# Two of the opening modulation products from rounded halves, ScalarE taking norm work, S5 eigenvalues moved into the head and the first retention moved behind the first gate

## The chip, the cores and the metric

The kernel runs on one core of one Trainium2 chip. The metric is device time in microseconds (us); shown is the median of three runs.

## The reference, cut to what matters

One layer of a hybrid decoder, for a prompt of 2048 rows and 64 sample rows (8 sequences of 8), width 1024, all in float32.

```python
mod = silu(c) @ w_ada + b_ada                      # 9 rows of c, w_ada 1024 x 6144
sh1, sc1, gt1, sh2, sc2, gt2 = split(mod, 6)
h = rms_norm(x, norm1_g) * (1 + sc1) + sh1
q, k, v, g, u, gate_r, gate_s = split(h @ w_in)    # 512 x5, 1024, 1024
ret = silu(g) * rms_normalize(retention(rotary(q), rotary(k), v))
lam_bar = exp(lam * exp(log_dt)); b_bar = ((lam_bar - 1) / lam) * b
ssm = gelu(s5_scan(u, lam_bar, b_bar, c, d)); ssm *= sigmoid(ssm @ w_glu)
x = x + gt1 * ((sigmoid(gate_r) * (ret @ w_br) + sigmoid(gate_s) * (ssm @ w_bs)) @ w_out)
x = x + gt2 * (relu((rms_norm(x, norm2_g) * (1 + sc2) + sh2) @ w_up)**2 @ w_down)
```

## The kernel before

The prompt is worked in four super-blocks of 512 rows. `setup` is the head: it computes the modulation columns that the first norm needs (`ada0` to `ada3`, 512 columns of `w_ada` each; 0 and 1 are the shift, 2 and 3 the scale), normalises the first 512 rows of x and leaves them transposed as `hh` (rounded to fp32r) and `hl` (what the rounding left), two tiles of four 128-row chunks each. Each super-block then multiplies by `w_in` in blocks of 512 columns, in the order u, q, k, v, g, gr0, gs0, gr1, gs1, and goes on with `glu`, the branches, the output product and the MLP. Between the blocks of super-block 0 lie the remaining modulation products `ada4` to `ada11`.

A weight unit is 256 rows by 512 columns. `fetch` (L180) issues its load from SP's queue into one of four buffers `wraw`; `refill` has ScalarE (ACT) round it to `whi` (L190) and GpSimd (POOL) form `wlo = wraw - whi` (L193; VectorE, DVE, for the `ada` units). Five `whi`/`wlo` pairs exist (the ring). Each block has four units, and each unit 24 products on TensorE (PE): for each of four row blocks j, two chunks by hi·hi, hi·lo, lo·hi (L252), into four PSUM banks of the tag `pd`. The banks are evacuated after the fourth unit, and the next block needs them: for q and k that is three DVE multiplications a bank (L1552 to L1554, `qU`, `rt`).

In the head `ada0` to `ada3` are plain float32 products of 9 columns (L848); DVE adds the bias (`ba`, L881), PE turns the sum (`ptm`, L886) and DVE copies it to `modT` (L887). ACT squares x (L639, two halves a row block), DVE scales x by its reciprocal root (L863) and modulates it (`m`, L688), ACT rounds it to `hh` (L690), POOL forms `hl` (L691). `ada4` on are products of a 41-row stationary that holds c rounded and its rest with `whi` and `wlo` (L258): ACT copies one part out (L903), DVE adds bias and the other part (L905, L906), PE turns it (L912).

S5 work stands in generators: `spawn` puts one beside the blocks, and it goes a step further at fixed counts of `tick`, which the blocks call; `finish` runs it to its end. `s5_setup` computes the eigenvalue functions on DVE (tiles `s5w`, L978 to L1058), powers (`s5pw`), tables (`s5ca`, `s5sa`, L1113 to L1125), then in eight steps the block matrices (L1142 to L1158, PE's `pw`, `pk`); it must end after block k. `s5(0, 4)` is then the first scan, to be ended before the retention of super-block 0 begins, beside gr0.

What the code writes is not yet the order of each engine: a modelled scheduler orders each engine's queue when the program is built, and the engine then executes it strictly in that order. Calls of `refill(True)` keep their written place.

Of the kernel before, what the change touches and what calls it, by code (L numbers as in the profile page):

```python
# [81 lines left out]
class Layer:  # L82
# [688 lines left out]
    def setup(self):  # L771
# [59 lines left out]
        pg = self.bank("pg", [P, 16])  # L831
        nc.tensor.transpose(pg, gn, self.ident[:16, :16])
        z = self.unit("z", shape=(P, 8, 41))
        V.memset(z, 0.0)
        V.tensor_copy(self.cT, z)
        V.tensor_copy(z[:, :, 0:9], pt)
        nc.scalar.activation(self.cT[:, :, 0:9], z[:, :, 0:9], AF.Copy)
        V.tensor_sub(self.cT[:, :, 32:41], z[:, :, 0:9], self.cT[:, :, 0:9])
        V.tensor_copy(self.gT.rearrange("p a k -> p (a k)"), pg)
# [35 lines left out]
        self.late_setup = self.s5_setup()
        next(self.late_setup)

    def mod_out(self, n, p, bias):
        nc = self.nc
        t = self.work("mt", [9, 512])  # L880
        nc.vector.tensor_add(t, p, bias)  # L881
        if n in (4, 5, 10, 11):
            nc.sync.dma_start(self.modd[:, 512 * n:512 * n + 512], t)
        pt = self.pd.tile([P, 4, 9], F32, tag="pd", name="ptm")
        for a in range(4):
            nc.tensor.transpose(pt[:, a], t[:, a * P:a * P + P], self.ident[:9, :9])  # L886
        nc.vector.tensor_copy(self.modT[:, 4 * n:4 * n + 4], pt)  # L887
# [40 lines left out]
    def s5_setup(self):  # L928
# [19 lines left out]
        bc = self.unit("s5bc", shape=(P, 4, G, 16))  # L948
        Bb, Bs, Cn, Cs = (bc[:, a] for a in range(4))
        for a, (x0, x1) in ((0, ("ssm_b_re", "ssm_b_im")), (1, ("ssm_b_im", "ssm_b_re"))):  # L950
            nc.sync.dma_start(bc[0:64, a], i[x0][0].rearrange("g p m -> p g m"))
            nc.sync.dma_start(bc[64:P, a], i[x1][0].rearrange("g p m -> p g m"))
        cc = self.unit("s5cc", shape=(P, 4, 2, 2, 64))
        for a, (x0, x1) in ((0, ("ssm_c_re", "ssm_c_im")), (1, ("ssm_c_im", "ssm_c_re"))):
            for h, nm in ((0, x0), (1, x1)):
                nc.sync.dma_start(cc[:, :, a, h], i[nm][0].rearrange("(f g) m p -> (g m) f p", f=4))
        dcol = cst.tile([P, G], F32, name="dcol")
        V.memset(dcol, 0.0)
# [870 lines left out]
```

## Time and profile before

| | |
|---|---|
| median of 3 runs | 3049.08 us (3045.45 to 3052.35) |
| the profiled execution | 3046.86 us, of it 3045.0 us span on the core |
| mean granted TensorE clock | 0.971 |
| PE busy | 2901.0 us (95%) |
| DVE, ACT, POOL busy | 1805.9 (59%), 1413.8 (46%), 1729.9 us (57%) |
| chain that ended last | PE 75%, DVE 13%, DMA 4%, POOL 3% |

Over the whole span PE is the bound; the chain's DVE share says that there are places where PE waits. The change touches the head and super-block 0 up to `glu`, the first 400 us.

### The profile page before, as it was taken

The numbers are of one execution on the slowest core, as the hardware profiler recorded it, in microseconds if no ns is written. First come the engines' busy times: TensorE is split into PE (matmuls) and PEld (weight loads), VectorE is DVE, ScalarE is ACT, GpSimd is POOL, SyncE is SP. The second block draws the span as 40 slices with busy tenths as digits, with TensorE's granted clock in tenths as the row PEclk, the third lists the DMA queues.
The fourth block names the chain that finished last, engine by engine and source line by source line (L and its number), as shares of the span: only waits on it lengthen the run. The fifth ranks groups of instructions, "written<-read, shape, count | busy, mean of one in ns | idle before, by whom it ended". The sixth has DMA issues, their size and how long they took to land.

```text
span 3045.0 us, 37372 instructions
## 1 busy us (share of the span) xinstructions
PE 2901.0 (95%) x13436; PEld 2374.9 (78%) x13436; DVE 1805.9 (59%) x2937; ACT 1413.8 (46%) x2296; POOL 1729.9 (57%) x1036
## 2 busy tenths in 40 slices
PE   8789999999999899999999999999999999999997
PEld 4568777788778788887788778887888788877886
DVE  6978544770575776365842645555556755545556
ACT  3223463322454334644344345556764555567643
POOL 3331355434254734564445487668777666689772
PEclk9889999999999999999999999999999999999999
DMA  8475435643226954447644455556545644457542
GB/s 266 137 219 188 127 129 176 182 114 119 77 95 204 289 177 118 139 166 228 194 129 149 163 185 185 189 196 209 181 153 175 208 167 152 153 197 241 191 149 97
DMA packets 337325, 518.62 MB, mean 170 GB/s; under 512 B 72038, under 2 KB 168822, under 8 KB 333035
## 3 DMA queue, kind: packets, MB, share of 16 engines
q1 hardware_dynamic: 337140, 516.24, 52.3%
q8 instruction: 106, 1.74, 0.2%
q14 instruction: 79, 0.65, 0.1%
HBM read 401.39 MB, written 114.78 MB: 170 GB/s over the span
## 4 chain that ended last, share of the span: by engine, by line
PE 75%; DVE 13%; DMA 4%; POOL 3%; issue 2%; ACT 2%; SPq 0%; ACTq 0%; DVEq 0%; POOLq 0%
PE pq_up L408 18%; PE pq_down L408 16%; PE pd_gr L252 6%; PE pd_gs L252 5%; PE pd_wo L252 4%; PE pd_br L252 3%; PE pd_u L252 2%; PE pd_g L252 2%; PE pd_bs L252 2%; PE pd_k L252 2%; PE pd_q L252 2%; PE pd_v L252 2%; PE pd_glu L252 2%; POOL tw L310 1%; DVE s5t L1226 1%
## 5 line engine op out<-in xcount | busy, mean ns | idle before, releaser
L193 POOL TENSOR_TENSOR wlo<-wraw,whi 128x1024 fp32r<-128x1024 f32 x248 | 623.2, 2525 | 714.2 <-ACT whi L190 600.5
L190 ACT ACTIVATE whi<-wraw 128x1024 fp32r<-128x1024 f32 x312 | 324.2, 1058 | 575.1 <-PE pd_wo L252 55.0
L408 PE MATMUL pq_down<-shi,tw 128*128 128x512 f32 x1792 | 562.1, 393 | 13.9 <-ACT acc L466 9.7
L408 PE MATMUL pq_up<-shi,tw 128*128 128x512 f32 x1792 | 557.6, 391 | 10.6 <-ACT tw L309 7.5
L408 PEld LDWEIGHTS pq_down<-shi,tw 128*128 128x128 f32 x1792 | 339.1, 189 | 86.7 <-ACT acc L466 10.5
L408 PEld LDWEIGHTS pq_up<-shi,tw 128*128 128x128 f32 x1792 | 338.3, 189 | 83.2 <-ACT tw L309 8.8
L310 POOL TENSOR_TENSOR tw<-traw,tw 128x512 fp32r<-128x512 f32 x192 | 277.8, 1459 | 142.7 <-ACT tw L309 142.5
L408 PE MATMUL pq_down<-slo,tw 128*128 128x512 f32 x896 | 351.8, 393 | 0.0
L408 PE MATMUL pq_up<-slo,tw 128*128 128x512 f32 x896 | 350.2, 391 | 0.0
L468 DVE SCALAR_TENSOR_TENSOR acc<-pq_down,modT,acc 128x512 f32<-128x512 f32 x224 | 162.4, 745 | 96.2 <-PE pq_down L408 95.9
L395 ACT ACTIVATE shi<-sw 128x1024 fp32r<-128x1024 f32 x140 | 147.2, 1058 | 152.8 <-DMA sw<-sd 100.2
L408 PEld LDWEIGHTS pq_down<-slo,tw 128*128 128x128 f32 x896 | 169.6, 189 | 34.4
L408 PEld LDWEIGHTS pq_up<-slo,tw 128*128 128x128 f32 x896 | 169.4, 189 | 34.6
L381 DVE TENSOR_TENSOR slo<-sw,far 128x512 fp32r<-128x512 f32 x160 | 103.8, 683 | 107.5 <-ACT far L380 92.2
L309 ACT ACTIVATE tw<-traw 128x512 fp32r<-128x512 f32 x224 | 137.8, 624 | 55.8 <-PE pq_down L408 38.4
L418 ACT ACTIVATE aq<-pq_up 128x512 f32<-128x512 f32 x128 | 72.7, 592 | 171.6 <-PE pq_up L408 171.6
L400 DVE TENSOR_TENSOR slo<-sw,shi 128x1024 fp32r<-128x1024 f32 x60 | 110.8, 1863 | 63.7 <-ACT shi L395 60.3
L193 DVE TENSOR_TENSOR wlo<-wraw,whi 128x1024 fp32r<-128x1024 f32 x64 | 90.9, 1421 | 74.3 <-ACT whi L190 69.9
L344 POOL TENSOR_TENSOR ts<-traw,ts 128x512 f32<-128x512 f32 x64 | 95.2, 1487 | 53.9 <-issue 48.9
L309 ACT ACTIVATE tw<-ts 128x512 fp32r<-128x512 f32 x128 | 80.2, 627 | 80.2 <-PE pq_up L408 70.9
L344 POOL TENSOR_TENSOR ts<-traw 128x512 f32<-128x512 f32 x64 | 87.3, 1365 | 45.6 <-DMA traw<-in_w_up_dram 27.3
L310 POOL TENSOR_TENSOR tw<-t,tw 128x512 fp32r<-128x512 f32 x64 | 89.9, 1412 | 40.0 <-ACT tw L309 39.9
(537 smaller groups left out, 6866.8 us busy)
## 6 DMA issues: line engine op xcount, KB each, us to landing
wraw<-in_w_in_dram SPq DMA_DIRECT2D x144, 512.0 KB
sw<-sd SPq DMA_DIRECT2D x112, 512.0 KB
s5p<-s5c SPq DMA_DIRECT2D x32, 1024.0 KB
traw<-in_w_up_dram SPq DMA_DIRECT2D x64, 512.0 KB
sd<-sq SPq DMA_DIRECT2D x32, 1024.0 KB
sd<-aq SPq DMA_DIRECT2D x32, 768.0 KB
traw<-in_w_down_dram SPq DMA_DIRECT2D x24, 1024.0 KB
wraw<-in_w_ada_dram SPq DMA_DIRECT2D x32, 512.0 KB
```

The source lines that it names most:

```text
L190: a = nc.scalar.activation(hi, raw, AF.Copy)
L193: l = eng.tensor_sub(lo, raw, hi)
L252: nc.tensor.matmul(banks[j], a, b, start=(k == 0 and z == 0), stop=(k == nk - 1 and z == 2))
L309: self.nc.scalar.activation(t[:, 0], x, AF.Copy)
L310: eng.tensor_sub(t[:, 1], x, t[:, 0])
L344: G.tensor_sub(x[p], l, x[m] if isinstance(m, int) else m)
L381: self.nc.vector.tensor_sub(d, a, c)
L395: nc.scalar.activation(hi[:, a], t, AF.Copy)
L400: V.tensor_sub(lo[:, a], t, hi[:, a])
L408: self.nc.tensor.matmul(bank, w, x, start=(first and a == 0 and z == 0), stop=(a == 3 and z == 2), skip_group_check=True)
L418: copy = lambda d, b: nc.scalar.activation(d, b, AF.Copy)
L468: V.scalar_tensor_tensor(d, b, g, d, op0=ALU.mult, op1=ALU.add)
```

## The change

- `b_ada` and the two norm gains come as one tile of 64 rows and one transpose; `modT` is set to the bias beforehand, and later sums are added to it (`sums`). The bias tile `ba` and the bias rows and additions of ada6 to ada9 go.
- `ada0` and `ada2` stay float32 products (`full`). `ada1` and `ada3` become 16 products each with `whi`/`wlo` halves (`split`, `halves`), whose rounding takes ring pairs, ACT time and, in turn, POOL and DVE time.
- Scaling x by its reciprocal root goes from DVE to ACT (`norm`, L892 after), as does the modulation of the first four chunks and of half of the others (L686 in place of L688).
- `ada3`'s sums and the second four chunks of `hh`/`hl` are made in `rest`, beside block u.
- `s5_setup` begins in the head: eigenvalues there, loads of B and C later. The rest of it and the first scan become one generator, `first_s5`, with shorter pauses, that must end after gr0; the retention of super-block 0 begins there.

```diff
+        gb = self.work("gb", [64, P])
+        dma(gb[0:48], raw_ap(i["b_ada"], 0, [[P, 48], [1, P]]))
...
         load(0)
-        self.x_rows(xu[0][:, 0], 0, 0)
-        dma(ba, raw_ap(i["b_ada"], 0, [[0, 9], [1, 2048]]))
-        self.x_rows(xu[0][:, 1], 0, 1)
+        self.x_rows(x[0], 0, 0)
+        next(s5)
+        self.x_rows(x[1], 0, 1)
         load(2)
         for j in range(2, 4):
-            self.x_rows(xu[1][:, j - 2], 0, j)
+            self.x_rows(x[j], 0, j)
         load(1)
+        self.fetch()
         load(3)
-        for _ in range(RAW):
+        for _ in range(RAW - 1):
...
+        V.tensor_copy(self.modT, pg[:, 0:48, None].to_broadcast([P, 48, 9]))
...
+        def split(n):
+            ws = []
+            for u in range(4):
+                raw = wa[2 * n + u // 2][:, 2 * (u % 2):2 * (u % 2) + 2]
+                hi = self.ring.tile([P, 2, 512], F32R, name="whi")
+                lo = self.ring.tile([P, 2, 512], F32R, name="wlo")
+                nc.scalar.activation(hi, raw, AF.Copy)
+                (V if u % 2 else nc.gpsimd).tensor_sub(lo, raw, hi)
+                ws.append((hi, lo))
+            return ws
+
+        def halves(n, ws):
+            pa = self.bank(f"ps_ada{n}", [P, 512])
+            for k in range(8):
+                for a in range(2):
+                    nc.tensor.matmul(pa[:41], self.cT[:, k], ws[k // 2][a][:, k % 2], start=(k == 0 and a == 0),
+                                     stop=(k == 7 and a == 1))
+            t = self.work("mt", [9, 512])
+            nc.scalar.activation(t, pa[32:41], AF.Copy)
+            V.tensor_add(t, t, pa[0:9])
+            return t
...
+        def sums(n, pt):
+            m = self.modT[:, 4 * n:4 * n + 4]
+            V.tensor_add(m, pt, m)
+            if n > 1:
+                self.scales(n)
+
+        def norm(j):
+            r = self.now(self.row_rstd(x[j]))
+            nc.scalar.activation(x[j], x[j], AF.Copy, scale=r)
...
-                for j in range(4):
-                    r = self.now(self.row_rstd(x[j]))
-                    V.tensor_scalar(x[j], x[j], r, None, op0=ALU.mult)
...
+            self.norm_out(pt, q, self.s1[:, :, 0], self.modT[:, 0:8, 0], self.hh, self.hl, j, nc.gpsimd, q and j % 2)
+        t = full(0)
+        norm(0)
+        next(s5)
+        norm(1)
+        sums(0, turn_mod(0, t))
+        pts = [turn(0, 0), turn(0, 1)]
+        next(s5)
+        t = full(2)
+        norm(2)
+        norm(3)
+        pts.append(turn(0, 2))
+        sums(2, turn_mod(2, t))
+        w1 = split(1)
+        for j in range(4):
+            out(pts[j] if j < 3 else turn(0, 3), 0, j)
+        next(s5)
+        self.refill(True)
+        t1 = halves(1, w1)
+        w3 = split(3)
+        pts = [turn(1, 0), turn(1, 1)]
+        sums(1, turn_mod(1, t1))
+        pts.append(turn(1, 2))
+        t3 = halves(3, w3)
+        self.refill(True)
+
+        def rest():
+            yield 2
+            p = turn_mod(3, t3)
+            yield 1
+            sums(3, p)
+            for j in range(2):
+                out(pts[j], 1, j)
+            yield 2
+            pts.append(turn(1, 3))
+            for j in range(2, 4):
+                out(pts[j], 1, j)
+            for _ in range(2):
+                self.refill(True)
+
+        self.late_setup = s5
+        self.rest = rest()
...
-            yield n // 5 + 1
+            yield n // 8 + 1
...
+    def first_s5(self):
+        yield from self.late_setup
+        yield 6
+        yield from self.s5(0, 4)
...
-            s5 = self.spawn(self.late_setup, 2)
+            self.spawn(self.rest, 1)
+            s5 = self.spawn(self.first_s5(), 5)
...
-        if b == 0:
-            self.finish(s5)
-            s5 = self.spawn(self.s5(b, 4), 13)
...
-        self.finish(s5)
-        rh, rl = self.unit("rh", F32R), self.unit("rl", F32R)
+        if b:
...
+            if not b and a == 0:
+                self.finish(s5)
+                rh, rl = begin()
```

Three places show what this makes of the engines' queues. On ACT, in the head, from the squares of x (`junk`) to the first half of u's first unit, before:

```order
L639 ACTIVATE junk,ss<-x_125 128x512 x4
L639 ACTIVATE junk,ss<-x_126 128x512 x4
L690 ACTIVATE hh<-m 128x4x128 x4
L190 ACTIVATE whi<-wraw 128x1024 x2
L690 ACTIVATE hh<-m 128x4x128 x4
```

and now (`x_126` holds row blocks 0 and 1, `x_127` blocks 2 and 3; `whi<-wa` are ada1's units, then ada3's; `ps_ada_303` is ada2's sum):

```order
L853 ACTIVATE mt<-ps_ada_303 9x512
L639 ACTIVATE junk,ss<-x_127 128x512 x2
L892 ACTIVATE x_126<-x_126,y 128x1024
L862 ACTIVATE whi<-wa 128x1024 x2
L639 ACTIVATE junk,ss<-x_127 128x512 x2
L862 ACTIVATE whi<-wa 128x1024 x2
L892 ACTIVATE x_127<-x_127,y 128x1024 x2
L686 ACTIVATE m<-pt,modT,s_108 128x128 x16
L690 ACTIVATE hh<-m 128x4x128 x4
L190 ACTIVATE whi<-wraw 128x1024
L862 ACTIVATE whi<-wa 128x1024 x4
L874 ACTIVATE mt<-ps_ada_438 9x512
```

ACT now has 16 modulations, four scalings and four roundings of `w_ada` ahead of u's first unit.

On PE, where `ada4` (`ps_ada_816` before, `ps_ada_858` now) stands against block u, before:

```order
L252 MATMUL pd_u<-hh,whi 128x512
L252 MATMUL pd_u<-hl,whi 128x512
L252 MATMUL pd_u<-hh,wlo 128x512
L258 MATMUL ps_ada_816<-whi,cT 41x512
L258 MATMUL ps_ada_816<-wlo,cT 41x512
```

and now:

```order
L252 MATMUL pd_u<-hh,wlo 128x512
L252 MATMUL pd_u<-hh,whi 128x512 x4
L258 MATMUL ps_ada_858<-whi,cT 41x512
L258 MATMUL ps_ada_858<-wlo,cT 41x512
L258 MATMUL ps_ada_858<-whi,cT 41x512
```

Before, ada4 stood behind the last product of u; now 12 of its 16 products stand ahead of the last 44 of u.

On DVE, at the evacuation of q's first two banks, before:

```order
L1148 TENSOR_TENSOR s5pk<-s5pk,s5bx 128x512
L1552 TENSOR_TENSOR qU<-pd_q,rot 128x512
L1553 TENSOR_TENSOR rt_1004<-pd_q,rot 64x512
L1554 TENSOR_TENSOR rt_1004<-pd_q,rot 64x512
L1142 TENSOR_TENSOR s5bx<-s5bc,s5pw 128x512
L1143 TENSOR_TENSOR s5bx<-s5bc,s5pw 128x512
L1145 TENSOR_TENSOR s5bx<-s5bc,s5pw 128x512
L1142 TENSOR_TENSOR s5bx<-s5bc,s5pw 128x512
L1143 TENSOR_TENSOR s5bx<-s5bc,s5pw 128x512
```

and now:

```order
L1175 TENSOR_TENSOR s5sa<-s5tm 128x32x32
L1190 TENSOR_TENSOR s5bc<-s5bc,s5pw 128x512
L193 TENSOR_TENSOR wlo<-wraw,whi 128x1024
L1177 TENSOR_SCALAR s5sa<-s5sa 64x2048
L1191 COPY s5bc<-s5bc 64x512
L1192 COPY s5bc<-s5bc 64x512
L1205 TENSOR_TENSOR s5bx<-s5bc,s5pw 128x512
L1207 TENSOR_TENSOR s5pk<-s5bc,s5pw 128x512
L1205 TENSOR_TENSOR s5bx<-s5bc,s5pw 128x512
L1207 TENSOR_TENSOR s5pk<-s5bc,s5pw 128x512
L1208 TENSOR_TENSOR s5bx<-s5bc,s5pw 128x512
L1622 TENSOR_TENSOR qU<-pd_q,rot 128x512
```

The eigenvalues are no longer among DVE's rows beside u, but the whole of the tables (`s5ca`, `s5sa`, before beside k) now stands ahead of q's evacuation.

Further on, on PE, the last step of the first S5 scan (`px`, L1212, and `py`, L1240 and L1241) stood among gr0's products before; now its last `px` and `py` stand between gr0's last product and gs0's first.

## Rows read from the trace of the kernel before

**Rows 1.** Busy time by stage: us, PE busy, PE's weight loads, DVE, ACT, POOL (instructions in brackets), granted clock, DMA share, GB/s. The stages are: the head, u with ada4, q, k, the rest of S5's setup with the start of v, the rest of v and g, the gates.
```profile
0.00:47.30 47.30, 36.27 (x121) 11.39 (x121) 21.37 (x76) 12.32 (x25) 10.27 (x10) 1.00 0.90 316
47.30:75.00 27.70, 27.70 (x126) 21.18 (x125) 26.93 (x97) 14.19 (x19) 12.53 (x7) 1.00 0.75 177
75.00:130.00 55.00, 37.10 (x152) 28.48 (x151) 54.38 (x127) 12.51 (x14) 25.06 (x12) 0.81 0.44 138
130.00:175.00 45.00, 41.34 (x191) 32.19 (x190) 44.06 (x69) 12.06 (x13) 17.10 (x9) 0.96 0.42 130
175.00:215.00 40.00, 31.25 (x145) 26.62 (x144) 26.69 (x44) 12.60 (x25) 2.54 (x2) 0.79 0.85 235
215.00:251.00 36.00, 33.37 (x191) 27.39 (x189) 32.32 (x69) 11.52 (x17) 10.26 (x4) 1.00 0.93 341
251.00:394.00 143.00, 136.24 (x697) 109.31 (x698) 86.78 (x187) 54.55 (x77) 49.38 (x23) 0.94 0.46 138
```
**Rows 2.** The waits of 47 to 394 us: engine, line, what it waited for: us in total, times, longest.
```profile
PE pd_k L252 <- DVE rt L1554: 10.2, 1, 10.2
PE pw L1154 <- DVE s5bx L1147: 8.0, 1, 8.0
```
**Rows 3.** The same columns as rows 1, for slices of 5 us around these waits.
```profile
85.00:90.00 5.00, 0.00 (x0) 0.00 (x0) 4.88 (x29) 0.00 (x0) 0.00 (x0) 0.50 0.00 0
90.00:95.00 5.00, 5.00 (x15) 4.07 (x16) 4.91 (x14) 0.00 (x0) 0.00 (x0) 0.52 0.53 153
115.00:120.00 5.00, 0.00 (x0) 0.00 (x0) 5.00 (x3) 0.59 (x1) 5.00 (x3) 0.87 0.53 136
190.00:195.00 5.00, 0.21 (x1) 0.24 (x2) 5.00 (x9) 0.00 (x0) 0.00 (x0) 0.54 0.81 308
195.00:200.00 5.00, 5.00 (x29) 5.00 (x29) 4.72 (x10) 1.20 (x2) 0.00 (x0) 0.50 0.00 0
```
**Rows 4.** The timeline of DVE and POOL beside u and q: start, us, engine, line, operation, output and input, count.
```profile
74.19 2.40 DVE L1033 TENSOR_SCALAR s5w<-s5w 128x64 f32<-128x64 f32 x1
83.67 0.21 DVE L989 SCALAR_TENSOR_TENSOR s5w<-s5w 128x64 f32<-128x64 f32 x1
72.29 11.27 POOL L193 TENSOR_TENSOR wlo<-wraw,whi 128x1024 fp32r<-128x1024 f32 x4 [12.19 <-ACT whi L190]
108.35 0.69 DVE L1553 TENSOR_TENSOR rt<-pd_q,rot 64x512 f32<-64x512 f32 x1
108.30 2.41 POOL L193 TENSOR_TENSOR wlo<-wraw,whi 128x1024 fp32r<-128x1024 f32 x1 [24.74 <-PE pw L1154]
```
**Rows 5.** The timeline of the head, PE (ada0, ada2, ada3; ada1 is left out; then u's first product) and ACT; same columns.
```profile
9.83 8.54 PE L848 MATMUL ps_ada<-wa,z 128*9 128x512 f32 x16 [1.25 <-DVE z L836]
19.48 7.04 PE L848 MATMUL ps_ada<-wa,z 128*9 128x512 f32 x16
...
39.16 7.03 PE L848 MATMUL ps_ada<-wa,z 128*9 128x512 f32 x16
47.31 0.50 PE L252 MATMUL pd_u<-hh,whi 128*128 128x512 f32 x1
21.66 0.63 ACT L639 ACTIVATE junk<-x 128x512 f32<-128x512 f32 x1 [5.42 <-DMA x<-in_x_prompt_dram]
38.69 1.99 ACT L190 ACTIVATE whi<-wraw 128x1024 fp32r<-128x1024 f32 x2
```
**Rows 6.** Groups of instructions of ACT, by line: count, busy us, mean ns of one, idle before and its releaser (the first over the whole span; the second for 0 to 251 us; the third is L666, the same operation as the moved scaling, later in the kernel: count, least, median and greatest ns, first and last start).
```profile
L686 ACT ACTIVATE m<-pt,modT,s 128x128 f32<-128x128 f32 x96 | 34.8, 468 | 13.5 <-PE pt L673 13.5
L190 ACT ACTIVATE whi<-wraw 128x1024 fp32r<-128x1024 f32 x41 | 42.1, 1055 | 72.9 <-DMA wraw<-in_w_ada_dram 21.4 <-PE pd_q L252 20.5 <-PE pd_v L252 20.1
L666 ACT ACTIVATE xr<-xr,y x12: 1132/1151/1154, 384.9 to 1312.4; 128x1024 f32<-128x1024 f32 x12
L690 ACT ACTIVATE hh<-m 128x512 fp32r<-128x512 f32 x8 | 5.1, 632 | 22.8 <-DVE m L688 22.8
```
**Rows 7.** POOL's products of 0 to 394 us, and a load that lands late: ACT's rounding of an ada unit and its wait.
```profile
L193 POOL TENSOR_TENSOR wlo<-wraw,whi 128x1024 fp32r<-128x1024 f32 x40 | 101.7, 2562 | 187.9 <-ACT whi L190 133.2 <-PE ps_ada L258 30.0 <-PE pw L1154 24.7
68.74 1.06 ACT L190 ACTIVATE whi<-wraw 128x1024 fp32r<-128x1024 f32 x1 [3.35 <-DMA wraw<-in_w_ada_dram]
```
**Rows 8.** PE's timeline at ada4, first and last product, and at the first products of gr0 and glu.
```profile
70.97 0.39 PE L258 MATMUL ps_ada<-whi,cT 128*41 128x512 f32 x1
74.41 0.40 PE L258 MATMUL ps_ada<-wlo,cT 128*41 128x512 f32 x1
249.81 0.50 PE L252 MATMUL pd_gr<-hh,whi 128*128 128x512 f32 x1 [1.20 <-DVE gU L1585]
398.36 0.98 PE L252 MATMUL pd_glu<-gh,whi 128*128 128x512 f32 x2 [0.18 <-ACT gh L1629]
```
**Rows 9.** DVE's timeline: the last evacuation of q and of k, two S5 products in a row and a `wlo`, the last three with no POOL work beside them.
```profile
127.69 0.68 DVE L1554 TENSOR_TENSOR rt<-pd_q,rot 64x512 f32<-64x512 f32 x1
162.95 0.68 DVE L1554 TENSOR_TENSOR rt<-pd_k,rot 64x512 f32<-64x512 f32 x1
187.35 0.68 DVE L1142 TENSOR_TENSOR s5bx<-s5bc,s5pw 128x512 f32<-128x512 f32 x1
187.95 0.68 DVE L1143 TENSOR_TENSOR s5bx<-s5bc,s5pw 128x512 f32<-128x512 f32 x1
132.45 1.21 DVE L193 TENSOR_TENSOR wlo<-wraw,whi 128x1024 fp32r<-128x1024 f32 x1
```

More of the change, by code (lines that the diff above doesn't have):

```diff
@@ L684, in norm_out @@
             k = 4 * q + a
-            if eng is nc.vector:
+            if not vec:
                 nc.scalar.activation(m[:, a], pt[:, a], AF.Identity, scale=s[:, k:k + 1], bias=b[:, k:k + 1])
@@ L830, in setup @@
             nc.tensor.transpose(pt[:, k], th[:, k * P:k * P + P], self.ident[:9, :9])
[L831 to L839, printed above, removed]
+        pg = self.bank("pg", [P, 64])
+        nc.tensor.transpose(pg, gb, self.ident[:64, :64])
+        z = self.work("z", [P, 8, 9])
+        zero = self.work("zero", [P, 8, 41])
+        V.memset(zero, 0.0)
+        V.tensor_copy(self.cT, zero)
+        V.tensor_scalar(z, pt, 0.5, None, op0=ALU.mult)
+        nc.scalar.activation(self.cT[:, :, 0:9], z, AF.Copy)
+        V.tensor_sub(self.cT[:, :, 32:41], z, self.cT[:, :, 0:9])
+        V.tensor_copy(self.modT, pg[:, 0:48, None].to_broadcast([P, 48, 9]))
+        V.tensor_copy(self.gT.rearrange("p a k -> p (a k)"), pg[:, 48:64])
         V.memset(self.R, 0.0)
@@ L873, in setup, with out @@
-        for _ in range(RING - 2):
-            self.refill(True)
[L875 to L887, printed above, removed]
+        def out(pt, q, j):
+            self.norm_out(pt, q, self.s1[:, :, 0], self.modT[:, 0:8, 0], self.hh, self.hl, j, nc.gpsimd, q and j % 2)
@@ L913, in evac @@
             yield 2
-            nc.vector.tensor_copy(self.modT[:, 4 * n:4 * n + 4], pt)
+            m = self.modT[:, 4 * n:4 * n + 4]
+            if rows:
+                nc.vector.tensor_copy(m, pt)
+            else:
+                nc.vector.tensor_add(m, pt, m)
             if n in (8, 9):
@@ L947, in s5_setup @@
         nc.sync.dma_start(ldt, raw_ap(i["ssm_log_dt"], 0, [[0, P], [1, G]]))
[L948 to L958, printed above, removed]
-        nc.sync.dma_start(dcol[112:P], i["ssm_d"][0].rearrange("g m -> m g"))
         yield
@@ L1029, in s5_setup @@
         yield
+        bc = self.unit("s5bc", shape=(P, 4, G, 16))
+        Bb, Bs, Cn, Cs = (bc[:, a] for a in range(4))
+        for a, (x0, x1) in ((0, ("ssm_b_re", "ssm_b_im")), (1, ("ssm_b_im", "ssm_b_re"))):
+            nc.sync.dma_start(bc[0:64, a], i[x0][0].rearrange("g p m -> p g m"))
+            nc.sync.dma_start(bc[64:P, a], i[x1][0].rearrange("g p m -> p g m"))
+        cc = self.unit("s5cc", shape=(P, 4, 2, 2, 64))
+        for a, (x0, x1) in ((0, ("ssm_c_re", "ssm_c_im")), (1, ("ssm_c_im", "ssm_c_re"))):
+            for h, nm in ((0, x0), (1, x1)):
+                nc.sync.dma_start(cc[:, :, a, h], i[nm][0].rearrange("(f g) m p -> (g m) f p", f=4))
+        dcol = cst.tile([P, G], F32, name="dcol")
+        V.memset(dcol, 0.0)
+        nc.sync.dma_start(dcol[112:P], i["ssm_d"][0].rearrange("g m -> m g"))
         for _ in range(3):
@@ L1129, in s5_setup @@
                               t.rearrange("p (s g) c -> p s (g c)", s=8))
+        for a, dst in ((0, Cn), (1, Cs)):
+            pc = self.bank("pc", [P, 4, P])
+            for f in range(4):
+                nc.tensor.transpose(pc[:, f], cc[:, f, a].rearrange("q h p -> q (h p)"), self.ident)
+            nc.scalar.activation(dst.rearrange("p g m -> p (g m)"), pc.rearrange("p f q -> p (f q)"), AF.Copy)
+        V.tensor_scalar(Cn[64:P], Cn[64:P], -1.0, None, op0=ALU.mult)
+        V.tensor_mul(t1, Bs, fi[:, :, None].to_broadcast(bsh))
+        V.tensor_mul(Bb, Bb, fr[:, :, None].to_broadcast(bsh))
+        V.tensor_add(Bb, Bb, t1)
+        V.tensor_copy(Bs[0:64], Bb[64:P])
+        V.tensor_copy(Bs[64:P], Bb[0:64])
         k0 = pw[:, 1536:2048].rearrange("p (g m) -> p g m", m=16)
@@ L1597, in super_block, with begin @@
             fr.append(self.spawn(self.retention_sample(zS, retS), 2))
-        fr.append(self.spawn(self.retention(b, qU, kU, vU, gU, rh, rl), 40 if smp else 2))
+        def begin():
+            rr = self.unit("rh", F32R), self.unit("rl", F32R)
+            fr.append(self.spawn(self.retention(b, qU, kU, vU, gU, *rr), 40 if smp else 2))
+            return rr
+        if b:
+            rh, rl = begin()
         gate = {}
@@ L1618, in super_block @@
             more_ada()
+            if not b and a == 0:
+                self.finish(s5)
+                rh, rl = begin()
         self.finish(*fr)
```

69 lines of the change are left out of this document (27 added, 42 removed).

## The prediction

> **What bounds the kernel now.** I read the table by stage first [rows 1]. In the head PE is busy 36.3 of 47.3 us; the DMA share of 0.90 says that weights and x are still coming in. Beside u PE has no gap at all. From 75 to 251 us it has many: the stages' idle times are 17.9, 3.7, 8.8 and 2.6 us, 33 us together, and the granted clock is 0.81 for q and 0.79 at 175 to 215 us. In the gates another 6.8 us are idle at a clock of 0.94. Over the same stages DVE is busy 54.4 of 55 and 44.1 of 45 us. So from q to the end of S5's setup DVE, not PE, sets the pace.
>
> The waits say it by name [rows 2]: k's first product waits 10.2 us for `rt`, the evacuation of q's bank on DVE, and `pw` 8.0 us for an S5 product on DVE. The slices [rows 3] add the price of a pause: PE is at 0 in 85 to 90 and 115 to 120 us, the clock is 0.50 right behind it, and 90 to 95 and 195 to 200 us are 100% busy at half clock, so each pause of 5 us costs up to 5 us more.
>
> DVE is slow there for a reason that the timeline shows [rows 4]. At 74.19 us a `s5w` operation of 128x64 takes 2.40 us while POOL forms four `wlo` (11.27 us); at 83.67 us, with POOL quiet, one takes 0.21. Of about 2.8 us of POOL DVE loses 2.2: 78%. An operation that reads a PSUM bank beside a `wlo` at 108.3 us takes its usual 0.69 us. The Trainium skill (SBUF — State Buffer, "Who interferes with whom") says why: a DVE instruction with two SBUF inputs, or in a 2-port mode, shares a locked port pair with POOL, for the whole instruction. These rows agree.
>
> **The head.** PE's own work shrinks: two float32 products of 7.03 us [rows 5] become two of 16 short products, which ada4 ran from 70.97 to 74.80 us [rows 8], 3.8 us each; ada3 moves into u. That would start u some 10 us sooner, were PE the bound. It is not: ada0 starts at about 9.5 us (before 9.83, one DVE step less), ada2 follows and ends at 25.9 (8.54 and 7.04 us and a gap). Only then does ACT's new queue run, in its fixed order: the copy of ada2 0.6; four squares 2.6 (0.63 each [rows 5], estimated up to 0.65); four scalings of x at 1.13, 4.5 [rows 6]; four roundings of ada1, 4.0 (two take 1.99 [rows 5]); sixteen modulations 5.8 (34.8 us for 96 [rows 6]); four `hh` 2.5; u's first rounding 1.0. Sum 21.0: u's first product comes at **46.9** against 47.31. The x squares could run sooner, x lands by 21.66 us [rows 5], but they stand behind the copy. Bounds: 38 (ACT's queue overlaps ada2) to 49. The eigenvalues that now stand on DVE in the head cost nothing: DVE is busy 21.4 of 47.3 us there [rows 1], they take about 15 without POOL; without that cover they would be 15 us ahead of the sums. The bias edits (four row loads, four additions) are under 1 us each beside other work: nothing.
>
> **Block u.** Ring pairs are short: ada1's four and u's first are all five, so ada3's roundings and u's next units follow one by one, and ACT's second rounding for u stands behind the copy of ada3. Hand chain: u's first unit waits for POOL's `wlo` (2.5 us [rows 7]) and ends at 55 at partly half clock; ada3 ends at 59.5; copy 0.6, rounding 1.06, `wlo` 2.5, then the second unit to 67.7; the last `hh` comes at 69.6. Twelve products of ada4 stand ahead of u's last 44: their raw load needs a buffer that POOL frees at 69.5, landing takes some 4 to 6 us (ACT waited 3.35 us for one [rows 7]), rounding and DVE's `wlo` 2.3: they end near 79. The 44 products (0.23 us each) and ada4's rest make it **92** against 74.8: 17 us later, of which 3.8 is ada3, the rest idle or slow PE. Bounds 84 to 98.
>
> **Block q and its evacuation.** q has no pause for the S5 work of 85 to 90 us, and ends at about 118. But q's banks are not free then: DVE stands at ada4's third `wlo` at about 82, and up to q's fourth evacuation its queue then holds 40 operations of 512 columns (0.60 from start to start [rows 9], 0.69 from PSUM: 25 us), 10 of 1024 (1.21: 12), one double one (2.2) and 48 small ones (0.2: 9): 48 us. POOL has some 14 us beside it; at 78% 11 us. Fourth bank out at **141**, against 128.4 [rows 9]; bounds 130 (no contention) and 146 (all of it and PE late). So PE waits some 20 us ahead of k, where it waited 10 before. What hides it: nothing.
>
> **k, v, g.** 72 more products of k (16.4 us) and the `pw`, `pk` pairs, which fall into this wait and no longer make the bunch of 195 to 213 us, end k near 172. DVE needs 33 us of its own and 9 of contention up to k's last evacuation: about 183, against 163.6 [rows 9]. From there DVE is light: the eigenvalues, tables and most of S5's matrices are behind it; some 31 us stand against v and g on PE, where the stages 175 to 251 had 59 [rows 1]. PE runs through: 43.7 for v and g, 7.6 for two modulation products, some 10 to 13 for S5's, from v's start at 181. gr0 begins at **245** against 249.8 [rows 8]: −5. Bounds 232 and 256.
>
> **The gates.** 250 to 398 us held 6.8 us of idle and 6% of low clock, 8.6 us [rows 1]. With S5's setup done, I give a third back, −5. Against it, the scan's last step stands ahead of gs0, a chain over ACT and DVE with little PE work beside it: +2. The retention begins some 35 us later, beside gs0 and gr1; the trace shows DVE light at the end of the gates (86.8 of 143 us over the stage), so this costs nothing unless it reaches `glu`. −3, bounds −12 and +12.
>
> **Sum.** −5 −3 = −8 us; behind `glu` the queues stand almost as before. Against the profiled execution 3046.9 − 8 = 3039; its time is 2.2 us under the median, so 3049.1 − 8 = **3041**.
>
> **Rivals.** *More gain:* DVE pays half of the contention, ACT's queue overlaps ada2, u begins at 39, q's last bank is out at 131, gr0 begins at 233, the gates give 6: −22, 3027. For it: PSUM readers are not slowed [rows 4], and there are 13 in the queue; against: the ring chain in u. *No change:* u's 17 us are not caught up; DVE's evacuation of k ends at 188, gr0 begins at 250, the gates keep their pauses: 3049. For it: DVE was the bound, and the queue from u to k loses only the eigenvalue rows, some of them already hidden. *The contention in full:* DVE loses 100% of POOL's time in place of 78%: 3 us more to q's last bank, 2 more to k's; gr0 begins at 250. Its time is that of the case before, and it shares its chance. The skill's rule named above, by which the lock is held for the whole instruction, would give this case. *Slower:* the tail of the first scan. `finish` now stands after gr0, and the last `px` and `py` stand alone ahead of gs0. If the scan is late (it starts later than before, since its tables do), PE waits there for the whole of a last step or two: two steps at some 5 us, then as much again at half clock, as 90 to 95 us shows [rows 3]: +20, in all +12, 3061. It decides where this wait with its slow clock passes 8 us. For it: DVE would have 38 us beside gr0's 40; against: v and g leave it time. That the change does less than it says is in the second case.
>
> **How the numbers follow.** Forecast 0.42 (3032 to 3047), more gain 0.14, no change 0.22, slower 0.22. A measurement of this kernel tells about 0.2%, 6 us, from no change. Faster: more gain and three quarters of the forecast's own range, 0.14 + 0.32, plus a little of the third, 0.48; same 0.28; slower 0.24. The range that leaves 2 in 10 out: 3020 to 3060.
>
> **What would show it.** Right: u's first product at 46 to 48 us; PE gaps inside u, ada4 ending near 92; one pause ahead of k, ended by `rt`, of some 20 us; no pause at 85 to 90 and none at 186 to 195 us; gr0 at 243 to 248. Wrong: a first product of u before 42 (ACT is not the bound); q's last evacuation before 135 or after 150 (DVE's queue mis-sized); a PE wait over 8 us ahead of gs0, or a retention that ends beside `glu`; any shift behind 400 us of over 3.

## The result, and the profile of the changed kernel

The changed kernel takes 3064.95 us (median of 4, 3060.11 to 3073.79), the kernel before beside it 3048.25: a ratio of 1.005, 95% interval 1.0035 to 1.0065. It is slower, by 16.7 us, where 3041 and a range up to 3060 were forecast. The two profiled executions differ as the medians do: 3063.85 − 3046.86 = 17.0 us.

The busy times by stage have the columns and stretches of [rows 1]:

```profile
0.00:47.30 47.30, 25.76 (x75) 8.83 (x76) 29.57 (x159) 21.68 (x44) 4.89 (x6) 0.82 0.86 310
47.30:75.00 27.70, 22.08 (x97) 14.98 (x95) 11.35 (x16) 13.19 (x25) 16.31 (x8) 0.93 0.15 41
75.00:130.00 55.00, 43.15 (x174) 31.41 (x172) 50.28 (x109) 20.53 (x26) 22.62 (x11) 0.88 0.62 170
130.00:175.00 45.00, 29.99 (x121) 22.87 (x122) 37.12 (x47) 9.14 (x11) 16.64 (x8) 0.73 0.38 122
175.00:215.00 40.00, 38.55 (x200) 30.57 (x198) 35.22 (x47) 14.38 (x21) 19.22 (x8) 1.00 0.63 213
215.00:251.00 36.00, 36.00 (x176) 28.81 (x175) 17.64 (x30) 13.34 (x21) 9.46 (x4) 1.00 0.99 306
251.00:394.00 143.00, 137.01 (x726) 114.01 (x725) 102.32 (x224) 53.70 (x79) 42.67 (x20) 0.93 0.48 150
```

From 175 us PE is as full as was hoped: 38.55 of 40 and 36.00 of 36 us at full clock, where [rows 1] had 31.25 at 0.79 and 33.37. PE's idle time lies ahead of that: 21.5 us in the head (before 11.0; two float32 products less stand there, and u starts 3.9 us later than before), 5.6 beside u (before none), and 15 in 130 to 175 us at a clock of 0.73 (before 3.7 at 0.96). The waits of PE from 47 to 415 us, in the columns of [rows 2], say for whom:

```profile
PE pd_k L252 <- DVE rt L1624: 16.6, 3, 10.9
PE ps_ada L258 <- DVE wlo L193: 4.3, 3, 2.9
PE pd_u L252 <- ACT hh L690: 3.2, 1, 3.2
PE py L1310 <- DVE s5t L1302: 2.8, 1, 2.8
```

It is the wait for q's evacuation again, 16.6 in place of 10.2 us; `pw` has 0.2 us in place of 8.0. The head's timeline, DVE and POOL, then ACT and PE (start, us, engine, line, operation, output and input, count, wait), shows where it begins:

```profile
29.91 2.30 DVE L1093 TENSOR_SCALAR s5w<-s5w 128x64 f32<-128x64 f32 x1
32.98 2.34 DVE L1100 TENSOR_TENSOR s5w<-s5w 128x32 f32<-128x32 f32 x1
...
29.81 2.35 POOL L863 TENSOR_TENSOR wlo<-wa,whi 128x1024 fp32r<-128x1024 f32 x1 [29.37 <-ACT whi L862]
32.93 2.34 POOL L863 TENSOR_TENSOR wlo<-wa,whi 128x1024 fp32r<-128x1024 f32 x1 [0.77 <-ACT whi L862]
...
38.13 1.15 ACT L892 ACTIVATE x<-x,y 128x1024 f32<-128x1024 f32 x1 [4.33 <-DVE s5w L1109]
41.42 1.15 ACT L892 ACTIVATE x<-x,y 128x1024 f32<-128x1024 f32 x1 [2.14 <-DVE s L951]
...
39.33 1.12 PE L898 MATMUL pt<-cpk,x 128*128 128x128 f32 x4 [9.84 <-ACT x L892]
51.23 1.19 PE L252 MATMUL pd_u<-hh,whi 128*128 128x512 f32 x4 [0.76 <-ACT whi L190]
```

The eigenvalue rows (`s5w`) stand on DVE among the few that make x's reciprocal root (`y`). Two of them, beside POOL's `wlo` of ada1, take 2.3 us each, as in [rows 4]. ACT waits 4.33 us for `y`, behind them in DVE's queue (the profile names the `s5w` row beside it; one `wlo` of ada1, 1.21 us, stands there too), and PE 9.84 for the scaled x. u starts at 51.2, not 46.9 us. In u it goes on; ACT, DVE and PE:

```profile
67.30 0.59 ACT L874 ACTIVATE mt<-ps_ada 9x512 f32<-9x512 f32 x1 [11.71 <-PE ps_ada L871]
71.60 2.91 ACT L686 ACTIVATE m<-pt,modT,s 128x128 f32<-128x128 f32 x8 [2.77 <-DVE s L952]
...
69.33 2.00 DVE L951 TENSOR_SCALAR s<-modT 128x36 f32<-128x36 f32 x1
79.45 4.87 DVE L193 TENSOR_TENSOR wlo<-wraw,whi 128x1024 fp32r<-128x1024 f32 x2 [5.13 <-ACT whi L190]
87.93 1.21 DVE L193 TENSOR_TENSOR wlo<-wraw,whi 128x1024 fp32r<-128x1024 f32 x1
...
78.53 2.07 PE L252 MATMUL pd_u<-hh,whi 128*128 128x512 f32 x4 [3.23 <-ACT hh L690]
89.19 0.65 PE L258 MATMUL ps_ada<-wlo,cT 128*41 128x512 f32 x1 [2.89 <-DVE wlo L193]
101.05 0.39 PE L252 MATMUL pd_u<-hh,wlo 128*128 128x512 f32 x1
```

Two things follow each other. The first is one serial chain: ada3's products, the copy (67.30), the sums and the scale (69.33), the second half of `m` (71.60) and `hh`, u's third unit (78.53). The second is ada4, whose 12 products stand next on PE: they take from 80.4 to 90.5 us, with 4.3 us of waits for their `wlo` on DVE and a clock of 0.50 from 80 to 90 us; the third `wlo` (87.93) has S5 rows ahead of it on DVE from 84.2 us on. Only then come u's last 44 products, the last at 101.1. From 40 to 75 us, while PE and ACT pass the work to and fro, DVE is busy 12.7 of 35 us (27.6 before): time that its later queue lacks. That queue ends with q's and k's last evacuations; then PE's first products of gr0 and `glu`:

```profile
150.71 0.68 DVE L1624 TENSOR_TENSOR rt<-pd_q,rot 64x512 f32<-64x512 f32 x1
199.07 0.68 DVE L1624 TENSOR_TENSOR rt<-pd_k,rot 64x512 f32<-64x512 f32 x1
...
260.39 0.48 PE L252 MATMUL pd_gr<-hh,whi 128*128 128x512 f32 x1
410.48 0.98 PE L252 MATMUL pd_glu<-gh,whi 128*128 128x512 f32 x2 [0.18 <-ACT gh L1707]
```

[Rows 9] have 127.69 and 162.95, and `glu` started at 398.36 [rows 8]. Of gr0 [rows 8] show the second piece; its first product was

```profile
247.43 0.48 PE L252 MATMUL pd_gr<-hh,whi 128*128 128x512 f32 x1
```

So of 17.0 us, 13.0 stand at gr0, −0.8 are added by the gates, and 4.9 behind `glu`.

### The profile page after: what moved, and what is told of

Same layout as the page of the kernel before. It is cut to its first block, busy times and chain, and to the rows that moved or that the text cites. A ratio compares the mean times of both kernels' runs of the same rounds, so it can differ in the third digit from the quotient of the medians.

```text
span 3062.1 us, 37372 instructions
## 1 busy us (share of the span) xinstructions
PE 2906.0 (95%) x13436; PEld 2382.4 (78%) x13436; DVE 1789.3 (58%) x2907; ACT 1436.3 (47%) x2336; POOL 1738.0 (57%) x1040
## 4 chain that ended last, share of the span: by engine, by line
PE 72%; DVE 13%; DMA 6%; ACT 4%; issue 3%; POOL 2%; SPq 0%; ACTq 0%; DVEq 0%; POOLq 0%
PE pq_up L408 17%; PE pq_down L408 12%; PE pd_gr L252 6%; PE pd_gs L252 5%; PE pd_wo L252 5%; DMA sw<-sd 3%; PE pd_br L252 3%; PE pd_u L252 2%; PE pd_k L252 2%; PE pd_g L252 2%; PE pd_q L252 2%; PE pd_bs L252 2%; PE pd_glu L252 2%; PE pd_v L252 2%; DVE s5t L1295 1%
## 5 line engine op out<-in xcount | busy, mean ns | idle before, releaser
L344 POOL TENSOR_TENSOR ts<-traw 128x512 f32<-128x512 f32 x64 | 86.9, 1357 | 46.9 <-DMA traw<-in_w_up_dram 28.6
```

The costliest lines, as they stand in the source:

```text
L344: G.tensor_sub(x[p], l, x[m] if isinstance(m, int) else m)
```

## The experiments

The times are medians, each beside runs of the kernel before on its own chip (medians 3049.1 to 3051.6); the places are from one profiled execution each. The times of one kernel scatter by up to 27 us in ten executions (e2, 3038.6 to 3065.4; the last section shows one place where that arises). The places up to `glu` agree within 1.2 us in two profiles of the kernel before, so they decide more than the medians do.

| kernel | u's first, last product (starts, us) | q's last evacuation | k's last product | gr0 | `glu` | time | ratio, interval |
|---|---|---|---|---|---|---|---|
| before | 47.3, 70.7 | 127.7 | 149.4 | 247.4 | 398.4 | 3048.25 | 1 |
| changed | 51.2, 101.1 | 150.7 | 189.0 | 260.4 | 410.5 | 3064.95 | 1.005 (1.0035 to 1.0065) |
| e1 | 45.2, 97.6 | 151.0 | 185.8 | 258.1 | 416.7 | 3069.4 | 1.0055 (1.0036 to 1.0073) |
| e2 | 45.4, 75.6 | 129.3 | 162.9 | 244.9 | 388.8 | 3051.2 | 1.000 (0.9982 to 1.0019) |
| e3 | 51.1, 96.2 | 146.0 | 178.0 | 250.2 | 394.6 | 3052.68 | 0.9999 (0.9982 to 1.0016) |
| e4 | 51.5, 102.2 | 152.3 | 184.3 | 270.4 | 413.9 | 3058.82 | 1.0025 (1.0015 to 1.0036) |
| e5 | 45.4, 79.0 | 128.6 | 161.8 | 239.7 | 386.8 | 3039.06 | 0.996 (0.9945 to 0.9975) |
| e6 | 50.7, 102.0 | 143.7 | 165.8 | 251.9 | 403.3 | 3055.43 | 1.0017 (1.0002 to 1.0031) |
| e7 | 46.3, 77.0 | 118.9 | 143.5 | 228.2 | 378.9 | 3032.03 | 0.9941 (0.9926 to 0.9956) |
| e8 | 50.6, 101.9 | 150.4 | 188.3 | 266.2 | 418.0 | 3064.45 | 1.0045 (1.003 to 1.0061) |
| e9 | 51.0, 96.7 | 151.0 | 189.2 | 270.4 | 413.9 | 3072.17 | 1.0076 (1.0049 to 1.0103) |
| e10 | 45.1, 77.7 | 117.5 | 143.6 | 227.9 | 377.8 | 3025.76 | 0.992 (0.9898 to 0.9943) |
| e11 | 45.0, 78.6 | 117.5 | 145.1 | 229.5 | 388.1 | 3037.89 | 0.9947 (0.9931 to 0.9964) |

**e1: the eigenvalues out of the head.**

```diff
         norm(0)
-        next(s5)
         norm(1)
...
         pts = [turn(0, 0), turn(0, 1)]
-        next(s5)
         t = full(2)
...
-        next(s5)
         self.refill(True)
```

> The changed kernel, but the S5 eigenvalue steps are not in the head; they begin beside block u, as before. Theory A (the eigenvalue rows stand between the rows of x's reciprocal roots on DVE, POOL's wlo stretches them, and ACT waits for the roots): ACT's waits of 4.3 and 2.1 us ahead of the last two scalings go, u's first product comes at 44 to 47 us instead of 51.2. What of that is left at the end depends on DVE: if u's pauses hide the eigenvalues there, glu comes 5 us sooner and the time is about 3060; if they delay q's evacuation as before, 3065 or more. Theory B (the ring chain in u sets the loss): u still lasts about 50 us.

The head is quicker, u starts at 45.2, 6.0 us earlier; nothing is left of it at q's last evacuation, and the time is not better. DVE's rows beside u, PE's wait in u and q's last evacuation:

```profile
71.54 2.37 DVE L1028 SCALAR_TENSOR_TENSOR s5w<-s5w 128x64 f32<-128x64 f32 x1
75.91 2.07 PE L252 MATMUL pd_u<-hh,whi 128*128 128x512 f32 x4 [5.11 <-ACT hh L690]
150.98 0.68 DVE L1621 TENSOR_TENSOR rt<-pd_q,rot 64x512 f32<-64x512 f32 x1
```

The eigenvalue rows now stand between the two halves of `m`; u's third unit waits 5.11 us. Their place in the head was wrongly priced, but moving them back beside u does not win the time back.

**e2: ada1 and ada3 as float32 products in the head.**

```diff
-        w1 = split(1)
...
-        t1 = halves(1, w1)
-        w3 = split(3)
+        t1 = full(1)
...
-        t3 = halves(3, w3)
+        t3 = full(3)
```

> The changed kernel, but ada1 and ada3 are float32 products in the head again (16 short passes of 7.0 us each), so they take no ring pairs and no rounding; the eigenvalues stay in the head, the second half of hh and hl stays beside u. Theory B (ada1's and ada3's halves hold the ring's five pairs, so that u's units come one by one): u lasts 28 to 33 us instead of 51 with ada4, q begins near 82 instead of 102, glu comes 12 to 20 us sooner than in the changed kernel, time 3045 to 3053. Theory A (late reciprocal roots in the head): u begins at 50 or later and nothing more is won, 3062 or more.

u ends at 75.6, 25 us earlier, q's last evacuation comes 21 earlier, gr0 15.5, `glu` 21.7, and the time falls by 14, to that of the kernel before. The halves carry most of the loss. u also starts at 45.4, though the eigenvalues still stand in the head. This edit takes away the chain through u, and four roundings and `wlo` for each of the two columns; it doesn't tell the one from the other.

**e3: x's scaling and all modulations back on DVE.**

```diff
-            nc.scalar.activation(x[j], x[j], AF.Copy, scale=r)
+            V.tensor_scalar(x[j], x[j], r, None, op0=ALU.mult)
...
-            self.norm_out(pt, q, self.s1[:, :, 0], self.modT[:, 0:8, 0], self.hh, self.hl, j, nc.gpsimd, q and j % 2)
+            self.norm_out(pt, q, self.s1[:, :, 0], self.modT[:, 0:8, 0], self.hh, self.hl, j, nc.gpsimd, True)
```

> The changed kernel, but x is scaled, and all of the first 512 rows are modulated, on DVE as before. Theory C (ACT's serial queue sets the head, as the prediction had it): u's first product comes about 8 us sooner, 43, and the time falls by up to 8 us to 3057. Theory A (DVE's queue with the eigenvalues sets it): DVE gets 4 x 0.74 and 24 x 0.33 us more, u begins at 50 or later, no gain, 3065 to 3070.

u starts no sooner, but ends 5 us sooner, gr0 comes 10 sooner and the time falls by 12: neither theory had that. DVE is hardly quicker at this work (0.33 us a modulation, ACT 0.36). But with `m` on DVE and `hh` on ACT side by side, POOL's first `hl` begins at 45.2 in place of 48.8 us, and u's first unit no longer waits for `hl` and `wlo` (1.4 and 2.1 us in the changed kernel). Of the 10 us at gr0, 5 are there at q's last evacuation and 11 at k's last product; where k gains the rest stays open.

**e4: S5's order of before.**

```diff
-            s5 = self.spawn(self.first_s5(), 5)
+            s5 = self.spawn(self.late_setup, 2)
...
+        if b == 0:
+            self.finish(s5)
+            s5 = self.spawn(self.s5(b, 4), 13)
...
-        if b:
-            self.finish(s5)
+        self.finish(s5)
...
-        if b:
-            rh, rl = begin()
+        rh, rl = begin()
...
-            if not b and a == 0:
-                self.finish(s5)
-                rh, rl = begin()
```

> The changed kernel, but S5's setup must again end after block k, the first scan after block g, and the retention of the first rows begins ahead of gr0; the eigenvalues stay in the head. If the later scan and retention are worth what they were meant to be, this is slower than the changed kernel: the setup bunches ahead of v again, with a pause and half clock of 10 us or more, 3075. If the gates gain nothing from the move, the time stays within 5 us of 3065.

gr0 comes 10.0 us later, the gates take 143.5 in place of 150.1, so `glu` starts 3.4 later; the median is 6 us lower all the same. The two signs contradict each other by less than the scatter: inconclusive. e11 asks part of the question again from a better base.

**e5: the edits of e2 and e3 together.**

> The changed kernel with ada1 and ada3 as float32 products in the head and with x scaled and all first rows modulated on DVE (the two edits of e2 and e3 together); the eigenvalues stay in the head, the S5 generator and the retention stay as changed. If the two costs add (ring chain, and ACT's queue beside u), glu comes 25 us sooner than in the changed kernel, 386 us, and the time is 3035 to 3042. If both edits remove the same loss, because DVE's queue from q to k is the bound behind either, glu stays at 388 to 392 and the time at 3048 to 3052.

`glu` at 386.8, 3039.06 us. At `glu` the sum of the two would be −37.5; together they give −23.6: by the places they remove in part the same lateness. The medians say that they add, −13.8 and −12.3 alone and −25.9 together, so this is not settled.

**e6: S5's generator begun later, beside u and q.**

```diff
-            s5 = self.spawn(self.first_s5(), 5)
+            s5 = self.spawn(self.first_s5(), 24)
```

> The changed kernel with one number changed: the S5 generator takes its first step beside the blocks after 24 counts instead of 5, so tables and block matrices begin one block later and stand behind q's evacuation on DVE. Theory D (from u's end on DVE's S5 rows ahead of q's and k's evacuation set the pace): k's wait for q's evacuation shrinks from 16.6 to under 8 us, k ends 8 to 12 us sooner, and what was put off finds DVE free beside v, g and gr0 (busy 18 of 35 us at 220 to 255); time 3053 to 3058. Theory E (the loss is all in the head and in u, the wait is only passed on): the S5 rows come back ahead of the gates, 3063 or more.

u is as late as in the changed kernel, but fewer S5 rows stand ahead of q's evacuation on DVE: it ends 7 us sooner, k 23, gr0 8.5. PE's waits from 47 to 225 us:

```profile
PE pd_v L252 <- DVE rt L1624: 9.2, 1, 9.2
PE pd_k L252 <- DVE rt L1624: 2.4, 1, 2.4
```

The wait has moved from k to v, and 15 of k's 23 us are lost again by gr0.

**e7: the edits of e2 and e6 together.**

> The changed kernel with ada1 and ada3 as float32 products in the head (e2) and the S5 generator's first step after 24 counts (e6). If ring chain and S5 rows are separate costs, this gains both: u ends at 75, q's last bank is out at 112 to 118 instead of 129, glu comes at 376 to 382, and the time is 3035 to 3042, below the kernel before. If the later S5 rows only move the wait to k or to the gates, glu stays at 388 and the time at 3050.

gr0 comes 32.2 us sooner than in the changed kernel, more than 15.5 and 8.5 together. In e2 S5's rows still stand between q's evacuations, and k waits 14.8 us in four pieces; in e6 u is still late; with both edits k waits for `rt` no more. At k's last product the two nearly add: 26.1 and 23.2 alone, 45.6 together. What makes the difference lies behind k, where the three kernels lose 10.6, 14.8 and 13.4 us again up to gr0. Each has one wait of v for k's evacuation, which the changed kernel does not have; e2's, then e7's:

```profile
PE pd_v L252 <- DVE rt L1622: 9.2, 1, 9.2
```

```profile
PE pd_v L252 <- DVE rt L1622: 10.2, 1, 10.2
```

Each edit alone meets this wait, and both together meet it once. In e6 and e7 S5 products that stood beside k also stand beside v. At `glu` the sum is nearly plain: 21.7 and 7.2 alone, 31.6 together.

**The kernel before, run again.**

> The kernel before itself, for a second profile of it. If the distances between the same places of two profiles are fixed, glu begins within 1 us of 398.4 and the distance from glu to the end is the same; if they scatter as the times of its runs do (3042 to 3058), the distance from glu to the end scatters by several us, and a shift behind glu of 5 us means nothing.

This run took 3063.85 us, with the places of before within 1.2 us up to `glu` (399.5); the last section reads it. Some 16 us of difference arise behind `glu`, 12 of them behind 2700 us, without any change in the kernel, so the 4.9 us behind `glu` in the result are not put down to the change.

**e8: ada1's and ada3's halves in buffers of their own, not the ring.**

```diff
-                hi = self.ring.tile([P, 2, 512], F32R, name="whi")
-                lo = self.ring.tile([P, 2, 512], F32R, name="wlo")
+                hl2 = self.unit("wsp", F32R)
+                hi, lo = hl2[:, 0:2], hl2[:, 2:4]
```

> The changed kernel, but the rounded halves of ada1 and ada3 lie in buffers of their own and not in the ring's five pairs; the order of ACT's queue is unchanged (u's second rounding still stands behind the copy of ada3). Theory B in its first form (too few pairs): u's pauses go, u with ada4 lasts 35 us instead of 51, time 3050. Theory F (it is the place in ACT's queue, not the pairs): u still lasts 49 to 52 us and the time stays at 3062 to 3067.

u ends at 101.9: the shortage of ring pairs, on which the prediction's chain through u rested, is not what holds u up.

**e9: u's second rounding ahead of ada3's on ACT.**

```diff
         t1 = halves(1, w1)
+        self.refill(True)
         w3 = split(3)
...
         t3 = halves(3, w3)
-        self.refill(True)
```

> The changed kernel with one line moved: u's second rounding stands ahead of ada3's four roundings instead of behind ada3's products; the ring is unchanged. Theory F: PE gets u's first two units in one piece, the 5 us of idle around 65 to 70 us go, but the second half of hh, which waits for ada3, comes no sooner: u ends 2 to 6 us earlier, time 3058 to 3063. If only the serial chain ada3, its sums, second half of hh counts: u ends where it did, at 101, or later, time 3065.

u ends 4 us sooner, q's last evacuation stays at 151.0, and the time is no better. The written place of this rounding is worth 4 us at u's end and nothing at q. What is left is the chain itself, from ada3's sum to `hh`, ada4's 12 products ahead of u's last 44, and DVE's queue behind them. That is by elimination: no run moves the chain or ada4's products alone.

**e10: the edits of e2, e3 and e6.**

> All three edits together: ada1 and ada3 as float32 products, x's scaling and modulation on DVE, the S5 generator's first step after 24 counts. If ACT's relief (e3) is a cost beside those of e7, glu comes at 372 to 377 us and the time is 3026 to 3030; if it was part of the chain in u that the float32 products already remove, it is that of e7, 3030 to 3034.

3025.76 us, ratio 0.992: it beats the changed kernel by 39 and the kernel before, beside it at 3051.09, by 25 us. q's last evacuation, gr0 and `glu`:

```profile
117.46 0.68 DVE L1622 TENSOR_TENSOR rt<-pd_q,rot 64x512 f32<-64x512 f32 x1
227.89 0.39 PE L252 MATMUL pd_gr<-hh,whi 128*128 128x512 f32 x1
377.81 0.98 PE L252 MATMUL pd_glu<-gh,whi 128*128 128x512 f32 x2 [0.18 <-ACT gh L1705]
```

Of the change it keeps the eigenvalues in the head, the sums on `modT`, S5's later end and the retention beside the later gates. `glu` is 20.6 us ahead of before, so 5 of the 25 lie behind it, inside the scatter. At `glu` it is 1.1 us ahead of e7: with the other two, e3's edit adds nothing that can be told.

**e11: e10 with the retention begun ahead of gr0.**

```diff
-        if b:
-            rh, rl = begin()
+        rh, rl = begin()
...
                 self.finish(s5)
-                rh, rl = begin()
```

> The kernel of e10 (float32 products for ada1 and ada3, norm work on DVE, S5 generator at the later pace), with one part of the change undone: the retention of super-block 0 begins ahead of gr0 again, not beside the later gates, while the end of the first scan stays behind gr0. Theory 1, the place of the retention is what e10 gains over the kernel before beyond the earlier q and k: DVE then has rotary and retention work beside gr0 and the last scan step comes later; gr0 and glu start 5 us or more later than in e10 (229.5, 377.8), and the time is 3031 or more. Theory 2, DVE is light in the gates in either order and nothing waits for the retention: glu starts within 3 us of 377.8, the time within 4 us of e10's 3026 (3022 to 3030).

gr0 starts 1.6 us later than in e10, `glu` 10.3: the gates take 158.6 in place of 149.9. The times differ by 12 us, the ratios by 0.0027 with intervals that just overlap (they ran on different chips). In e11, PE's last product of gs0 and the retention's last product, then slices of 5 us of the gates in the columns of [rows 3]:

```profile
304.68 0.39 PE L252 MATMUL pd_gs<-hh,wlo 128*128 128x512 f32 x1
306.80 0.63 PE L1417 MATMUL prt<-cpk,rw 128*128 128x128 f32 x4 [1.73 <-DVE rw L1413]
...
305.00:310.00 5.00, 3.27 (x23) 2.96 (x22) 4.87 (x10) 1.58 (x2) 2.80 (x1) 0.86 0.83 295
310.00:315.00 5.00, 5.00 (x24) 4.82 (x23) 3.83 (x12) 0.80 (x2) 0.00 (x0) 0.50 0.87 310
315.00:320.00 5.00, 2.50 (x12) 2.34 (x11) 4.83 (x16) 0.00 (x0) 0.00 (x0) 0.50 0.50 90
320.00:325.00 5.00, 5.00 (x24) 5.00 (x25) 4.91 (x17) 0.39 (x1) 0.00 (x0) 0.50 0.29 44
325.00:330.00 5.00, 5.00 (x26) 5.00 (x25) 4.82 (x16) 2.66 (x6) 0.00 (x0) 0.50 0.00 0
330.00:335.00 5.00, 5.00 (x16) 2.85 (x16) 3.13 (x11) 2.76 (x5) 0.68 (x1) 0.50 0.00 0
```

PE pauses at 305 us, and from 310 us the clock is at 1.2 GHz for 25 us. Up to 338.5 us, where gr1 begins, PE has only the last half of the scan (32 of 64 `px`, their `py`) and products of an `ada`, with DVE busy beside them. In e10 the same scan steps stand beside gs0 (`px` from 271 to 298 us), 8 us lie between gs0 and gr1 in place of 34, and one slice is at 0.50. So with the retention ahead of gr0 the scan's last steps come later and stand alone; beginning it behind gr0 is worth some 10 us at `glu`, on this base.

## Why the prediction was wrong

**The head.** It said that the eigenvalues "cost nothing", and counted DVE's busy time against the stage's length. Their place counts: they stand between x's root rows, and POOL's `wlo`, which the change puts there too, stretches them: +4.3 us at u's start. It takes both: u starts at 45 with the rows out (e1), and also with the rows there and the halves out (e2). e1 shows that the gain is gone at q's last evacuation.

**Block u.** The forecast had its lateness, 92 with ada4, and it was 102.4 (four of ada4's products follow u's last). Of the missing 10 us, 4.3 come from the head. u's first unit took 11.4 in place of 8 us, with waits of 1.4 us for `hl` and 2.1 for `wlo`. From there to the second unit's end the hand chain held (12.7 us, forecast 12.7). From that to the end of ada4's 12 products it took 15.2 us, forecast 11.3: their `wlo` came late, at a clock of 0.50. Of the reasons given, the ring pairs were wrong (e8), and the written order on ACT explains 4 us at u's end and none at q (e9).

**q's evacuation.** Its length nearly holds: from ada4's third `wlo` to the fourth bank 59 us were forecast, 87.93 to 151.4 is 63.5. What failed more is its start, 82 against 87.9. With the late start and 4.5 us of its own the bank came at 151.4, not 141, and past the bound of 146.

**k.** From that bank to k's end 31 us were forecast; it took 38. The four banks come out 2 to 6 us apart, and PE waits three times for them at a clock of 0.73 for the stage. So k ended at 189, 17 us later than forecast.

**v and g.** This step held: k's end to gr0 is 71 us (forecast 73, before 98). The pauses behind k are gone, as said. That was in part luck: the 73 held 9 us in which v waits for k's evacuation; here v did not wait for it, and took more than forecast from its start to gr0 (67.5 us, forecast 64). But the sum took 25 us of gain and 22 of lateness at k's end; the lateness was 39.6. This lateness at k's end is the term that was mis-sized, and it turns the sign. The step from there to −5 also used 249.81 as gr0's start; from its first product, 247.43, the same 245 is −2.4.

**The gates.** Forecast −3, measured −0.8. The scan's tail costs a wait of 2.8 us for `py` and 15 us at half clock (270 to 285 us), so the rival *slower* was there in a small form; it did not decide. The prediction gave the moved retention no price; e11 shows a gain, on another base.

**The rivals.** 3061 of *slower* is near the time, but by another mechanism. *No change* named the right one, "u's 17 us are not caught up", with k's evacuation ending at 188; it ended at 199.8.

## What to carry to other kernels

Work moved under another engine's time is not hidden because that engine has idle time in the stage; look at what stands right behind it in the same queue, and who waits for that. When a product moves from a busy stage into a later one, write down the chain from its result to the next product that needs it, and carry its end through every in-order queue behind it. A gain read at one place can be lost again at the next wait, so try edits together before giving up on either: at k's end −26 and −23 became −46, at gr0 −15.5 and −8.5 became −32, because what is lost behind k is lost once.
